# Gating of a mixture of experts in three operations instead of six, none of them on GpSimd

## The chip, the cores and the metric

The kernel runs on one core of a Trainium2 chip. The metric is the device time of one execution in microseconds (us). TensorE multiplies matrices, VectorE and ScalarE work on elements, GpSimd (Pool) does so too and issues the indirect transfers, SyncE issues most of the other transfers.

## What is computed

The reference runs two transformer-like blocks over 512 tokens of width 1024. The first block (two layers of convolution, a recurrent scan and a feed-forward) and the attention part of the second are not touched by the change. The part that matters here is the last stage, a mixture of 32 experts of which every token takes 4:

```python
u = (xb @ w1[e] + b1[e]).astype(jnp.float32)
glu = jnp.minimum(u[:, 0::2], SWIGLU_LIMIT)               # 7.0
lin = jnp.clip(u[:, 1::2], -SWIGLU_LIMIT, SWIGLU_LIMIT)
act = glu * jax.nn.sigmoid(SWIGLU_ALPHA * glu) * (lin + 1.0)   # alpha 1.702
y = act.astype(xb.dtype) @ w2[e] + b2[e]
return y.astype(jnp.float32) * g[:, None]
```

The even columns of `u` are the gate, the odd ones the linear part. The result is weighed by the token's gate, by a modulation row (`mod[:, 5]`, `M5` in the kernel) and added to the token.

## The kernel before

**One expert.** Experts are taken in a fixed order of rank by load. Each has a fixed number of rows (`CAPS`): rank 0 has 128, ranks 1 and 2 have 192 in two blocks, ranks 3 to 9 have 128, ranks 10 to 15 have 96, ranks 16 to 31 have 64. `ORDER` puts some 64-row experts first, then the two of 192, then those with 128, those with 96, and the other ten with 64. `up` (L1886) multiplies the gathered rows by the first matrix, 8 steps of 128 rows of weights (`kt`) into four PSUM banks `pu` of 512 columns; `down` (L1919) multiplies the gated result by the second into two banks `py`.

**Precision.** Each block of weights arrives by a transfer of 1 MB (`stage`, eight buffers in turn). `split_big` (L1782) makes of it a rounded copy `mh` on ScalarE (L1785) and the rest `ml` on VectorE (L1786); TensorE multiplies both parts (L1834). Up to 64 rows, a block is packed: the high and the low part of the rows lie side by side, and some steps (`PLAIN`) use the unsplit weights (L1829). The result of a packed block has two halves, which `whole` (L1840) joins with a copy on ScalarE and an addition on VectorE into SBUF; that of a wider block is read from PSUM as it is.

**Gating.** `gated` (L1874) works on one bank, 256 gate and 256 linear columns. VectorE clips the gate columns into `glu` (L1879) and the linear ones into a spare tile (L1880), ScalarE takes the Sigmoid (L1881), and Pool multiplies (L1882), adds 1 (L1883) and multiplies again (L1884). There are 34 blocks of rows and so 136 such units; in the second half of the last expert, two units, VectorE does Pool's part. Then `Rows(g, "a")` transposes `glu` on TensorE, eight transposes a block of rows (L1817), and copies them into two parts (L1819, L1821, L1822) for `down`.

**Order.** In the program text, the transposes of an expert's `glu` stand in the next expert's `up`, at `kt == 3`, and `down` after that; the rows of the next expert but one are gathered meanwhile (L1868, an indirect transfer that Pool issues), and results are added to the output by another (L1916). The text is not the final order. Before the run, the framework lays out the queue of each engine from its own estimates of durations, moving an instruction ahead of others where its inputs are expected; in the trace most transposes of `glu` stand earlier than `kt == 3`. At run time each engine takes its queue in order.

**Ahead of the experts.** L1772 to L1780 load the row `M5` and the biases of all experts and split the biases into a rounded part and a rest, `BB`, which is added by a matmul (L1838).

Of the kernel before, what the change touches and what calls it, by code (L numbers as in the profile page):

```python
# [16 lines left out]
AF = mybir.ActivationFunctionType  # L17
OP = mybir.AluOpType
# [10 lines left out]
CH = 64  # L29
STG = 8  # L30
ATC = 2
MB, LB = 3, 2

PLAIN = ((1, 4), (1, 2))
# [92 lines left out]
def tile_two_blocks(ctx: ExitStack, tc: tile.TileContext, I: dict, out: bass.AP, dump=None, stop=None):  # L127
    nc = tc.nc
# [16 lines left out]
    def bank(kind, shape, name):  # L145

        ring = dict(mm="AAAC", sq="BBDD", iv="A", pg="A", pp="B", py="C", sm="D", yy="B", tr="D", ad="A", s="EEE", w="F", o="G", t="HH", pv="I",
                    pre="EEEHH")[kind]
        turn[kind] = turn.get(kind, -1) + 1
        t = ring[turn[kind] % len(ring)]  # L150
        return ps.tile(shape or [128, 512], F32, name=name, tag="bank" + t, bufs=banks[t])

    def mmps(shape=None, name="mm"):
        return bank("mm", shape, name)
# [4 lines left out]
    def f32(ap):  # L159
        return ap.bitcast(F32)  # L160
# [541 lines left out]
    def scan(l, S):  # L702
# [66 lines left out]
        def conv_out(m):  # L769

            if m % 2 == 0 or not wcs:
                wcs[m // 2] = load_w(I["w_out"][l], 0, 4, (m // 2) * 256, 256)
            o = XT[:, m]
            if m < AHEAD_M:
                o = wk.tile([128, TT], F32, name="xm", tag="acc", bufs=1)
                nc.sync.dma_start(o[:, 0:w], xd[:, m * TT:m * TT + w])
            for i, (a, n) in enumerate(SEG[:1] if l == 1 else SEG):
                p = bank("pg", None, "pco")
                for kt in range(4):
                    nc.tensor.matmul(p[:, 0:n], lhsT=wcs[m // 2][:, kt, m % 2 * 128:m % 2 * 128 + 128], rhs=S["CV"][kt][:, a:a + n], start=kt == 0, stop=kt == 3)  # L780
                yield
                gated(o[:, a:a + n], p[:, 0:n], S["MOD"][:, i, 16 + m:17 + m], l == 1 and a < TX)
            if m < AHEAD_M:
                nc.sync.dma_start(xd[:, m * TT:m * TT + w], o[:, 0:w])
            yield
# [306 lines left out]
    def gated(o, src, gate, perm):  # L1092

        if perm:
            src = src.rearrange("p (c r) -> p r c", r=8)
            o = o.rearrange("p (r c) -> p r c", r=8)
        nc.vector.scalar_tensor_tensor(o, src, gate, o, op0=OP.mult, op1=OP.add)

    def proj_add(wsrc, nk, h, gates, both, perm, r0=0, after=None, parts=None):

        def add(m, p, a, n, gate):
            gated(XT[:, m, a:a + n], p[:, 0:n], gate[:, m:m + 1], perm and a < TX)

        for m2 in range(0, KT, 2):
            t = load_w(wsrc, r0, nk, m2 * 128, 256)
            if parts and m2 == KT - 2:
                ws = [split_w(t, i * 128, 128) for i in range(2)]
                ps_ = [[mmps(name="pp") for _ in parts] for i in range(2)]
                for j, (a, n) in enumerate(parts):
                    for i in range(2):  # L1110
                        mm3(ws[i], h, nk, [(ps_[i][j], a, n)], 128)
                        add(m2 + i, ps_[i][j], a, n, gates[a >= TX])
                continue
            for i in range(2):
                m = m2 + i
                sg = segs(both)
                mm3(split_w(t, i * 128, 128), h, nk, sg, 128)
                for s, (p, a, n) in enumerate(sg):
                    add(m, p, a, n, gates[s])
                if after:  # L1120
                    after(m)
# [128 lines left out]
    def win2(c0, n):  # L1250
        t = load_w(win, 0, KT, c0, n)
        return lambda i, m=128: split_w(t, i * 128, m)

    first = []
    with tc.high_priority():
        f = win2(256, 160)
# [24 lines left out]
    f = win2(0, 256)  # L1281
    for i in range(2):
        p_tile(f, i, 128, False, P1[:, i])
    f = win2(672, 256)
    for i in range(2):
        p_tile(f, i, 128, True, P1[:, 3 + i], 64 ** -0.5)
    f = win2(416, 256)
    for i in range(2):
        p_tile(f, i, 128, False, P1[:, 5 + i])
    for j in range(0, 4, 2):  # L1290
        f = win2(928 + j * 128, 256)
        for i in range(2):
            p_tile(f, i, 128, True, P2[:, j + i])
    for j in range(0, 4, 2):
        f = win2(1440 + j * 128, 256)
# [25 lines left out]
    for t in range(6):  # L1321
        p = bank("pre", None, "rvt")
# [63 lines left out]
    for t in range(4):  # L1386
        for a, n in SEG:
            p = bank("pre", None, "pq")
# [8 lines left out]
    p = bank("w", None, "ppe")  # L1397
# [9 lines left out]
    for t in range(6):  # L1407
        r = LAT[:, 4 + t:5 + t]
        for i in range(2):
            p = bank("pre", None, "pkv")  # L1410
# [14 lines left out]
    for t in range(4):  # L1425
        q = QT[:, t].rearrange("p (h c) -> p h c", h=8)[:, :, 64:96]
        o = wk.tile([128, 8, 32], F32, name="qpe", tag="qpe", bufs=1)
        turned(o, q, tables[0], t, 8)
        nc.scalar.activation(q, o, AF.Copy)
    for t in range(6):  # L1430
        rk = SS[:, 4 + t]
        k, kp = KTL[t], KP[:, t:t + 1]
        if t < 4:
            o = wk.tile([128, 1, 32], F32, name="kpe", tag="kpe", bufs=1)
            turned(o, kp, tables[1], t, 1)
        else:
            o = kp
# [137 lines left out]
    for h in range(4):  # L1575
        o = MO[:, 4 + h]
# [47 lines left out]
    def row_of(n, dst):  # L1624

        nc.scalar.dma_start(dst, bass.AP(tensor=CD.tensor, offset=CD.offset + n * D, ap=[[0, 128], [1, D]]))
# [12 lines left out]
    def stage(src, parts=1, eng=nc.sync):  # L1639
        t = stages[stages_used[0] % STG]  # L1640
        stages_used[0] += 1
        if parts > 1:
            t = t.rearrange("p (a b) -> p a b", a=parts)
        eng.dma_start(t, src)
        return t
# [28 lines left out]
    for t in range(4):  # L1674
        xr = XR[t // 2][:, t % 2]
        for c in range(2):
            p = mmps(name="prow")
# [84 lines left out]
    M5 = wk.tile([128, D], F32, name="M5")  # L1762
    XF = XT.rearrange("p k t -> p (k t)")
    spare = [XF[:, D * i:D * i + D] for i in range(6)]
    turn = dict(xg=0, y=0)

    def ring(kind):

        turn[kind] += 1
        return spare[2 * (kind == "y") + turn[kind] % 2]  # L1770

    row_of(2, M5)  # L1772

    BB = wk.tile([64, 3072], F32R, name="BB")
    bt = XF[0:32, 2 * D:5 * D]
    stages.extend(wk.tile([128, 2048], F32, name=f"st{i}") for i in range(6, STG))
    for src, c0, n in ((I["b_mlp1_2"][0], 0, 2048), (I["b_mlp2_2"][0], 2048, 1024)):
        nc.gpsimd.dma_start(bt[:, c0:c0 + n], src)
        nc.scalar.activation(BB[0:32, c0:c0 + n], bt[:, c0:c0 + n], AF.Copy)
        nc.vector.tensor_tensor(BB[32:64, c0:c0 + n], bt[:, c0:c0 + n], f32(BB[0:32, c0:c0 + n]), op=OP.subtract)  # L1780

    def split_big(t):  # L1782
        wh = wk.tile([128, 2048], F32R, name="mh", tag="mh", bufs=MB)
        wl = wk.tile([128, 2048], F32R, name="ml", tag="ml", bufs=LB)
        nc.scalar.activation(wh, t, AF.Copy)  # L1785
        nc.vector.tensor_tensor(wl, t, f32(wh), op=OP.subtract)  # L1786
        return wh, wl
# [83 lines left out]
    def glus(xs):  # L1871
        return [wk.tile([128, D], F32, name="glu", tag="glu", bufs=2)[0:x.m] for x in xs]

    def gated(x, p, i, glu, c, f, eng=nc.gpsimd):  # L1874

        u = x.whole(p, i).rearrange("p (f two) -> p two f", two=2)
        o = glu[:, c:c + 256]
        lin, sg = (spare[i][0:x.m, f:f + 256] for i in (4, 5))
        nc.vector.tensor_scalar(o, u[:, 0], 7.0, None, op0=OP.min)  # L1879
        nc.vector.tensor_scalar(lin, u[:, 1], 7.0, -7.0, op0=OP.min, op1=OP.max)  # L1880
        nc.scalar.activation(sg, o, AF.Sigmoid, scale=1.702)  # L1881
        eng.tensor_tensor(sg, o, sg, op=OP.mult)  # L1882
        eng.tensor_scalar(lin, lin, 1.0, None, op0=OP.add)  # L1883
        eng.tensor_tensor(o, lin, sg, op=OP.mult)  # L1884

    def up(w1, x, lb, out, at=(lambda kt: None)):  # L1886

        pu = [mmps(name=f"pu{n}") for n in range(4)]
        cols = [n * 512 for n in range(4)]
        for kt in range(KT):  # L1890
            if first:
                w = first.pop(0)
            else:
                t = early.pop(0) if early else stage(w1(kt))
                w = (t,) if x.packed and kt in PLAIN[0] else split_big(t)
            x.into(pu, w, kt, cols, [(lb, c) for c in cols], kt == KT - 1)
            at(kt)
        return [lambda n=n: gated(x, pu[n], n, out, n * 256, n * 256) for n in range(4)]

    def up_half(w1, xs, lb, h, out, at=(lambda kt: None)):  # L1900

        pu = [mmps(name=f"pu{n}") for n in range(2 * len(xs))]
        for j in range(KT // 2):
            w = split_big(stage(w1(j, h), 2).rearrange("p a b -> p (a b)"))
            for i in range(2):
                for b, x in enumerate(xs):
                    x.into(pu[2 * b:2 * b + 2], w, 2 * j + i, [i * 1024, i * 1024 + 512], [(lb, h * 1024), (lb, h * 1024 + 512)], j == 3 and i == 1)
                at(2 * j + i)
        return [lambda n=n: gated(xs[n // 2], pu[n], n, out[n // 2], h * 512 + n % 2 * 256, n * 256, nc.vector if len(xs) == 1 and h else nc.gpsimd) for n in range(2 * len(xs))]

    def weighed(y, x, p, n, c, tok, end):

# [168 lines left out]
    xs = [Rows(b[2], "x") for b in got[0][0]]  # L2081
    got[1] = place(ORDER[1])
    before, acts = None, []
    for i in range(33):
        steps = [None]
        if i < 32:
# [5 lines left out]
            out = glus(xs)  # L2092
# [15 lines left out]
        for step in steps:  # L2108
# [5 lines left out]
            for k in range(nparts):  # L2114
# [4 lines left out]
                if k < 2 and (i != 31 or not end):  # L2119
                    for _ in range((len(acts) + 1 - k) // (2 - k)):  # L2120
                        acts.pop(0)()
                if end and k == (ATC if nparts == 4 else 1) and i < 31:
                    xs = [Rows(b[2], "x") for b in got[i + 1][0]]
# [8 lines left out]
    with tc.For_i(0, nov, 1) as v:  # L2132
# [5 lines left out]
        x = Rows(xg, "x")  # L2138
        glu = glus([x])
# [36 lines left out]
```

## Time and profile before

| | |
|---|---|
| time, median of 3 runs | 4156.53 us (4144.9, 4156.53, 4166.9) |
| the profiled execution | 4152.49 us |
| its span, first to last instruction | 4150.5 us |
| mean granted clock of TensorE | 0.952 |
| busy: TensorE, VectorE, ScalarE, Pool | 92%, 68%, 41%, 21% of the span |
| the expert stage | from about 2740 us to the end |

Busy shares are means over very different stages. In the tables below, PE is TensorE, PEld its loading of weights, DVE VectorE, ACT ScalarE, POOL GpSimd, SP SyncE. Times are us from the start of the span, unless marked ns. PEclk is the clock that TensorE was granted, as a share of full speed. A row `out<-in` names the tiles that are written and read.

### The profile page before, as it was taken

Reading aid. Unit: us, or ns where it says so; the run is one execution under the profiler, and the core shown is the slowest. Engines: PE = TensorE matmul, PEld = TensorE weight load, DVE = VectorE, ACT = ScalarE, POOL = GpSimd, SP = SyncE. Lnnn points to the kernel's source line nnn. Section 1 sums busy time; section 2 is a strip of 40 time slices with the busy share of each in tenths; the row PEclk is TensorE's granted clock in tenths of the full one; section 3 lists DMA queues with packets and bytes.
Section 4 is the critical chain, followed back from the end, with each engine's and each line's share of the span. In section 5 each row is a group of like instructions: output and inputs, shape, how many; then the busy total and the mean of one; then the engine's idle time right before and its main releaser. Section 6 shows DMA issues by size and latency. Waiting matters only on the chain. (4 is left out here: it accounts for less than half of the span.)

```text
span 4150.5 us, 70327 instructions
## 1 busy us (share of the span) xinstructions
PE 3828.5 (92%) x27963; PEld 2860.0 (69%) x27963; DVE 2812.5 (68%) x5538; ACT 1710.6 (41%) x2552; POOL 873.9 (21%) x703
## 2 busy tenths in 40 slices
PE   7998999999999988999999989979999999888997
PEld 5777776888888777777878866754556776554343
DVE  4778875743434879867555545577687999677776
ACT  3233352321212334533222434445455766545554
POOL 0001110000000001110000000025566678545343
PEclk8999999999999999999999998989999999899899
DMA  5122423432322211125454310248697999778886
GB/s 200 53 70 65 133 54 104 133 119 85 122 81 92 73 48 33 41 60 164 156 160 129 77 51 1 107 176 309 242 339 277 365 360 348 270 274 311 300 334 219
DMA packets 353982, 677.90 MB, mean 163 GB/s; under 512 B 118759, under 2 KB 230194, under 8 KB 323538
## 3 DMA queue, kind: packets, MB, share of 16 engines
q1 hardware_dynamic: 343024, 636.89, 44.2%
q0 software_dynamic: 9376, 34.63, 3.4%
q8 instruction: 221, 3.62, 0.4%
q10 hardware_dynamic: 1250, 1.85, 0.1%
q14 instruction: 111, 0.91, 0.1%
HBM read 635.39 MB, written 37.90 MB: 162 GB/s over the span
## 5 line engine op out<-in xcount | busy, mean ns | idle before, releaser
L429 ACT ACTIVATE wh<-wst 128x1024 fp32r<-128x1024 f32 (+2 forms) x222 | 222.7, 1004 | 983.1 <-PE pc L439 524.3
L1786 DVE TENSOR_TENSOR ml<-E,mh 128x2048 fp32r<-128x2048 f32 x236 | 552.3, 2352 | 111.3 <-PE pu L1834 49.4
L1785 ACT ACTIVATE mh<-E 128x2048 fp32r<-128x2048 f32 x236 | 447.4, 1914 | 188.6 <-PE pu L1834 151.7
L439 PE MATMUL px<-Hh,wl 128*128 128x512 f32 (+2 forms) x1216 | 485.2, 399 | 13.9 <-DVE wl L430 13.7
L439 PE MATMUL px<-Hh,wh 128*128 128x512 f32 (+3 forms) x1216 | 484.5, 400 | 13.4 <-ACT wh L429 7.1
L439 PE MATMUL px<-Hl,wh 128*128 128x512 f32 (+3 forms) x1216 | 484.7, 399 | 1.0 <-DVE Hl L417 0.8
L430 DVE TENSOR_TENSOR wl<-wst,wh 128x1024 fp32r<-128x1024 f32 (+2 forms) x222 | 255.8, 1154 | 266.6 <-ACT wh L429 263.9
L1834 PE MATMUL pu<-ml,ch 128*64 128x512 f32 (+2 forms) x968 | 278.5, 406 | 20.5 <-DVE ml L1786 20.3
L1883 POOL TENSOR_SCALAR XT<-XT 64x256 f32<-64x256 f32 (+2 forms) x134 | 202.8, 1515 | 431.4 <-DVE XT L1880 414.5
L1834 PE MATMUL pu<-mh,ch 128*128 128x512 f32 (+1 forms) x968 | 282.5, 407 | 1.1 <-ACT ch L1819 1.0
L439 PEld LDWEIGHTS px<-Hh,wl 128*128 128x128 f32 (+1 forms) x1216 | 231.0, 190 | 72.6 <-DVE wl L430 18.9
L439 PEld LDWEIGHTS px<-Hh,wh 128*128 128x128 f32 (+1 forms) x1216 | 231.2, 191 | 72.0 <-ACT wh L429 9.4
L1006 POOL TENSOR_SCALAR XT<-XT,PC 128x64 f32<-128x64 f32 x160 | 85.3, 544 | 885.8 <-DVE XT L1009 370.7
L439 PEld LDWEIGHTS px<-Hl,wh 128*128 128x128 f32 (+1 forms) x1216 | 230.8, 190 | 56.8 <-DVE Hl L417 4.9
L531 DVE SCALAR_TENSOR_TENSOR acc<-ZC,VT,acc 128x272 f32<-128x272 f32 (+2 forms) x600 | 254.3, 485 | 2.6 <-ACT acc L526 2.5
L1786 DVE TENSOR_TENSOR ml<-st,mh 128x2048 fp32r<-128x2048 f32 x86 | 201.5, 2353 | 75.0 <-PE pu L1834 32.3
L1834 PEld LDWEIGHTS pu<-mh,ch 128*128 128x128 f32 (+1 forms) x968 | 174.4, 187 | 82.5 <-issue 31.7
L1834 PEld LDWEIGHTS pu<-ml,ch 128*64 128x64 f32 (+2 forms) x968 | 151.3, 161 | 91.3 <-DVE ml L1786 32.0
L1884 POOL TENSOR_TENSOR glu<-XT 64x256 f32<-64x256 f32 (+2 forms) x134 | 200.9, 1501 | 7.4
L439 PE MATMUL pc<-Hh,wh 128*128 128x256 f32 x672 | 193.3, 288 | 0.9 <-ACT Hh L416 0.9
L1882 POOL TENSOR_TENSOR XT<-glu,XT 64x256 f32<-64x256 f32 (+2 forms) x134 | 192.2, 1437 | 3.3 <-ACT XT L1881 3.2
L439 PE MATMUL pc<-Hl,wh 128*128 128x256 f32 x672 | 192.1, 286 | 0.5 <-DVE Hl L417 0.5
(599 smaller groups left out, 8487.2 us busy)
## 6 DMA issues: line engine op xcount, KB each, us to landing
E<-in_w_mlp_dram SPq DMA_DIRECT2D x288, 1024.0 KB
st<-in_w_mlp_dram SPq DMA_DIRECT2D x94, 1024.0 KB
wst<-in_w_in_dram SPq DMA_DIRECT2D x29, 1024.0 KB
adt<-in_ada_w_dram SPq DMA_DIRECT2D x96, 256.0 KB
adt<-in_w_ada_dram SPq DMA_DIRECT2D x96, 256.0 KB
wst<-in_ffn_wg_dram SPq DMA_DIRECT2D x22, 1024.0 KB
wst<-in_ffn_wu_dram SPq DMA_DIRECT2D x22, 1024.0 KB
adaw<-in_ada_w_dram SPq DMA_DIRECT2D x16, 1024.0 KB
```

Source lines behind the costliest of these rows:

```text
L429: nc.scalar.activation(wh, t[:, :, c0:c0 + n], AF.Copy)
L430: nc.vector.tensor_tensor(wl, t[:, :, c0:c0 + n], f32(wh), op=OP.subtract)
L439: nc.tensor.matmul(p[0:m, 0:n], lhsT=wa[:, k, 0:m], rhs=ha[:, k, a:a + n], start=k == 0 and first, stop=k == nk - 1 and last)
L531: nc.vector.scalar_tensor_tensor(o, z[:, j + a:j + a + n], cw(j), o, op0=OP.mult, op1=OP.add)
L1006: nc.gpsimd.tensor_scalar(M[:, 1], M[:, 0], PC[:, c:c + 1], None, op0=OP.mult)
L1785: nc.scalar.activation(wh, t, AF.Copy)
L1786: nc.vector.tensor_tensor(wl, t, f32(wh), op=OP.subtract)
L1834: nc.tensor.matmul(p[0:xa.shape[2]], lhsT=xa[:, kt], rhs=w[part][:, c:c + 512], start=kt == 0 and j == 0, stop=last and j == len(parts) - 1)
L1882: eng.tensor_tensor(sg, o, sg, op=OP.mult)
L1883: eng.tensor_scalar(lin, lin, 1.0, None, op0=OP.add)
L1884: eng.tensor_tensor(o, lin, sg, op=OP.mult)
```

## The change

`gated` takes Silu of 1.702 times the gate column on ScalarE straight from `u`, which is 1.702 times the gate times its sigmoid; VectorE clips the linear column to -6 and 8, and one scalar_tensor_tensor on VectorE limits the Silu to its value at 7 (`SILU7`) and multiplies by the linear part. For this the 1 of `lin + 1` goes into the bias of the odd columns, and the factor 1.702 is taken out again by dividing `M5` by it and multiplying the second bias by it. Each unit thus has one operation on ScalarE and two on VectorE, and none on Pool.

```diff
--- before.py
+++ after.py
@@ -29,6 +29,8 @@
 CH = 64
 STG = 8
 ATC = 2
+ALPHA = 1.702
+SILU7 = 7 * ALPHA / (1 + math.exp(-7 * ALPHA))
 MB, LB = 3, 2
 
 PLAIN = ((1, 4), (1, 2))
@@ -1769,13 +1771,20 @@
         turn[kind] += 1
         return spare[2 * (kind == "y") + turn[kind] % 2]
 
+
     row_of(2, M5)
+    nc.vector.tensor_scalar(M5, M5, 1.0 / ALPHA, None, op0=OP.mult)
 
     BB = wk.tile([64, 3072], F32R, name="BB")
     bt = XF[0:32, 2 * D:5 * D]
     stages.extend(wk.tile([128, 2048], F32, name=f"st{i}") for i in range(6, STG))
     for src, c0, n in ((I["b_mlp1_2"][0], 0, 2048), (I["b_mlp2_2"][0], 2048, 1024)):
         nc.gpsimd.dma_start(bt[:, c0:c0 + n], src)
+        odd = bt[:, 1:2048:2]
+        if c0:
+            nc.vector.tensor_scalar(bt[:, c0:c0 + n], bt[:, c0:c0 + n], ALPHA, None, op0=OP.mult)
+        else:
+            nc.vector.tensor_scalar(odd, odd, 1.0, None, op0=OP.add)
         nc.scalar.activation(BB[0:32, c0:c0 + n], bt[:, c0:c0 + n], AF.Copy)
         nc.vector.tensor_tensor(BB[32:64, c0:c0 + n], bt[:, c0:c0 + n], f32(BB[0:32, c0:c0 + n]), op=OP.subtract)
 
@@ -1871,17 +1880,14 @@
     def glus(xs):
         return [wk.tile([128, D], F32, name="glu", tag="glu", bufs=2)[0:x.m] for x in xs]
 
-    def gated(x, p, i, glu, c, f, eng=nc.gpsimd):
+    def gated(x, p, i, glu, c, f):
+
 
         u = x.whole(p, i).rearrange("p (f two) -> p two f", two=2)
-        o = glu[:, c:c + 256]
-        lin, sg = (spare[i][0:x.m, f:f + 256] for i in (4, 5))
-        nc.vector.tensor_scalar(o, u[:, 0], 7.0, None, op0=OP.min)
-        nc.vector.tensor_scalar(lin, u[:, 1], 7.0, -7.0, op0=OP.min, op1=OP.max)
-        nc.scalar.activation(sg, o, AF.Sigmoid, scale=1.702)
-        eng.tensor_tensor(sg, o, sg, op=OP.mult)
-        eng.tensor_scalar(lin, lin, 1.0, None, op0=OP.add)
-        eng.tensor_tensor(o, lin, sg, op=OP.mult)
+        o, lin = glu[:, c:c + 256], spare[4][0:x.m, f:f + 256]
+        nc.scalar.activation(o, u[:, 0], AF.Silu, scale=ALPHA)
+        nc.vector.tensor_scalar(lin, u[:, 1], 8.0, -6.0, op0=OP.min, op1=OP.max)
+        nc.vector.scalar_tensor_tensor(o, o, SILU7, lin, op0=OP.min, op1=OP.mult)
 
     def up(w1, x, lb, out, at=(lambda kt: None)):
 
@@ -1906,7 +1912,7 @@
                 for b, x in enumerate(xs):
                     x.into(pu[2 * b:2 * b + 2], w, 2 * j + i, [i * 1024, i * 1024 + 512], [(lb, h * 1024), (lb, h * 1024 + 512)], j == 3 and i == 1)
                 at(2 * j + i)
-        return [lambda n=n: gated(xs[n // 2], pu[n], n, out[n // 2], h * 512 + n % 2 * 256, n * 256, nc.vector if len(xs) == 1 and h else nc.gpsimd) for n in range(2 * len(xs))]
+        return [lambda n=n: gated(xs[n // 2], pu[n], n, out[n // 2], h * 512 + n % 2 * 256, n * 256) for n in range(2 * len(xs))]
 
     def weighed(y, x, p, n, c, tok, end):
```

## Rows read from the trace of the kernel before

**Rows 1.** List of waits, 2750 to 4151 us: us in total, times, longest.
```profile
PE pcol L1817 <- POOL glu L1884: 79.9, 39, 5.6
...
ACT XT L1881 <- DVE glu L1879: 73.2, 71, 2.6
```

**Rows 2.** List of waits, 2750 to 2950, 3474 to 3716, 3716 to 4088.
```profile
PE pcol L1817 <- POOL glu L1884: 19.3, 6, 5.6
...
PE pcol L1817 <- POOL glu L1884: 34.9, 13, 4.6
...
PE py L1834 <- DVE ml L1786: 4.3, 4, 1.2
...
PE pcol L1817 <- POOL glu L1884: 25.6, 19, 3.7
```

**Rows 3.** Table by stretch: us; busy us (x instructions); PEclk, DMA share, GB/s.
```profile
2740.00:2774.00 34.00, 10.28 (x43) 7.68 (x43) 31.60 (x86) 13.74 (x14) 16.47 (x13) 0.60 0.66 237
...
3214.00:3437.00 223.00, 223.00 (x1024) 176.46 (x1023) 216.52 (x214) 157.98 (x122) 158.85 (x82) 1.00 0.97 363
...
3763.00:4088.00 325.00, 295.67 (x966) 132.81 (x964) 237.81 (x271) 170.04 (x176) 140.80 (x112) 0.92 0.86 322
```

**Rows 4.** Timeline, a 96-row and a 64-row expert: start, us, instruction, [idle before <-releaser].
```profile
3547.82 0.41 DVE L1879 TENSOR_SCALAR glu<-pu 96x256 f32<-96x256 f32 x1
...
3556.38 0.39 PE L1817 MATMUL pcol<-CF,glu 96*128 96x96 f32 x2 [4.47 <-POOL glu L1884]
...
3965.70 0.34 PE L1817 MATMUL pcol<-CF,glu 64*128 64x64 f32 x2 [1.89 <-POOL glu L1884]
```

**Rows 5.** Table by stretches of 2 us behind that last wait.
```profile
3966.00:3968.00 2.00, 2.00 (x13) 1.03 (x11) 0.89 (x2) 1.92 (x5) 1.50 (x1) 0.68 0.97 387
3968.00:3970.00 2.00, 2.00 (x5) 0.73 (x4) 0.73 (x2) 2.00 (x3) 0.00 (x0) 0.50 1.06 291
3970.00:3972.00 2.00, 2.00 (x4) 0.67 (x4) 2.00 (x1) 2.00 (x2) 0.00 (x0) 0.50 0.37 92
3972.00:3974.00 2.00, 2.00 (x5) 0.47 (x4) 0.26 (x1) 1.53 (x1) 0.00 (x0) 0.62 0.04 8
```

**Rows 6.** Timeline of TensorE: the bias matmul near each expert's start.
```profile
3436.71 1.17 PE L1838 MATMUL pu<-BB,lb 64*96 64x512 f32 x4
...
3473.97 1.17 PE L1838 MATMUL pu<-BB,lb 64*96 64x512 f32 x4
...
3715.96 1.13 PE L1838 MATMUL pu<-BB,lb 64*64 64x512 f32 x4
...
4087.99 0.67 PE L1838 MATMUL pu<-BB,lb 64*64 64x512 f32 x2
```

**Rows 7.** Single lines of the kernel: duration ns min/median/max, first and last start, forms.
```profile
L1167 ACT ACTIVATE ft<-pc x22: 367/376/378, 785.0 to 1280.0; 128x256 f32<-128x256 f32 x22
L1167 ACT ACT_TABLE_LOAD  x3: 1283/1283/1283, 776.8 to 2223.4; - x3
...
L1786 DVE TENSOR_TENSOR ml<-E,mh x236: 2272/2289/2827, 2764.9 to 4120.5; 128x2048 fp32r<-128x2048 f32 x118
...
L1879 DVE TENSOR_SCALAR glu<-cl x72: 272/281/816, 2827.1 to 4124.4; 64x256 f32<-64x256 f32 x72
...
L1880 DVE TENSOR_SCALAR XT<-pu x64: 408/416/422, 2794.6 to 3695.5; 128x256 f32<-128x256 f32 x40, 96x256 f32<-96x256 f32 x24
...
L1882 DVE TENSOR_TENSOR XT<-glu,XT x2: 410/413/416, 4124.8 to 4125.7; 64x256 f32<-64x256 f32 x2
...
L1914 DVE SCALAR_TENSOR_TENSOR XT<-cl,ix,M x36: 733/738/1222, 2887.8 to 4138.0; 64x512 f32<-64x512 f32 x36
```

**Rows 8.** Timeline of ScalarE in a 128-row expert.
```profile
3310.32 1.90 ACT L1785 ACTIVATE mh<-st 128x2048 fp32r<-128x2048 f32 x1
3312.12 0.40 ACT L1881 ACTIVATE XT<-glu 128x256 f32<-128x256 f32 x1
```

**Rows 9.** The page, transfers: issues, KB each (the stage's other 96 are alike).
```profile
E<-in_w_mlp_dram SPq DMA_DIRECT2D x288, 1024.0 KB
```

## The prediction

> **What bounds the kernel now.** The kernel has many stages, so I read the waits before any share of busy time. In the expert stage (about 2740 us to the end) the list of waits [rows 1] shows which gaps of TensorE are named after the edited code: the transposes of `glu` at L1817 stood still 39 times, 79.9 us in all, for the last Pool operation of the gating, L1884. The reader is also to see the row below it: ScalarE waits 73.2 us for VectorE's first clip, L1879. ScalarE is not the bound, so that one is no price.
>
> Next, where these waits are. The same list cut into stretches [rows 2] gives 19.3 us in the first experts, 34.9 in the experts with 96 rows and 25.6 in the late ones with 64 rows: all of it. The table by stretch [rows 3] shows what limits where the waits are absent: from 3214 to 3437 us (128 rows) TensorE is busy all 223 us at full clock, VectorE 216.5 of 223, and the transfers run at 363 GB/s. From 3763 to 4088 us (64 rows) the clock is 0.92, VectorE is busy 73% and the transfers run at 322 GB/s: nothing there is full.
>
> Then one expert in order of time [rows 4]. In the 96-row expert VectorE begins the first clip at 3547.82, but the transposes of that block, for which TensorE had stood 4.47 us, start only at 3556.38: 8.5 us later, with the block's three Pool operations in between. In the 64-row experts the last block costs 1.89 us, and right behind it the granted clock falls [rows 5]: 0.68, 0.50, 0.50, 0.62 over four slices of 2 us. The lost clock is 2 x (0.32 + 0.50 + 0.50 + 0.38) = 3.4 us. A wait thus costs more than its length.
>
> **The change, part by part.** *Pool's three operations go.* There are 136 blocks of gating (72 packed with 64 rows, 64 wider), and 134 of them used Pool. What comes back is the wait plus the clock behind it, stretch by stretch.
>
> 96 rows: the starts of the experts [rows 6] give an undisturbed period, 3473.97 - 3436.71 = 37.3 us. The next five take 3715.96 - 3473.97 = 242.0 us, 55.7 us more than 5 x 37.3. Of this 4.3 us are waits for `ml` [rows 2], which stay. That leaves 51 us: the 34.9 of waits and half as much again for the clock. I take 46, leaving 1 us an expert for a shorter wait in the same place.
>
> 64 rows: nine experts from 3715.96 to 4087.99 take 41.3 us each [rows 6]. Waits 25.6 [rows 2], and nine falls of the clock at 3.4 [rows 5], 31, make 57 us, or 35.0 us an expert. (A clock of 0.92 over 325 us [rows 3] is 26 us in eight experts, the same size.) Each expert fetches 12 blocks of 1024 KB [rows 9], 12.6 MB; at 35.0 us that is 360 GB/s, as much as the best long stretch [rows 3]. I take three quarters, 43 us (36.6 us an expert, 344 GB/s), because the transfers would otherwise have to sit at that level throughout.
>
> First experts: 19.3 us of waits [rows 2]; the clock behind them is not counted; I take 15, since VectorE is also full of one-time work there. The gains add up to 46 + 43 + 15 = 104 us; everything at its full price would be 51 + 57 + 29 (19.3 with half again for the clock, as in the 96 rows) = 137. Nothing is taken for the 128-row experts, where TensorE has no gap to give back.
>
> *VectorE: one clip goes, one scalar_tensor_tensor comes.* The clip from SBUF takes 0.281, the one from PSUM 0.416 [rows 7]. The new operation has two SBUF inputs of 256 columns. The nearest rows are the product of L1882 on VectorE, 64 x 256, 0.413, below, and a scalar_tensor_tensor of 512 columns, 0.738, above [rows 7]. I take 0.47, close to the lower one, as the columns are the same. So 72 x 0.19 + 64 x 0.05 = 17 us more on VectorE; at the lower end 72 x 0.13 = 10, at the upper 72 x 0.46 + 64 x 0.32 = 54. The late experts leave VectorE a quarter of the time free [rows 3], and that is the cover; without it all 17 would show. I put a quarter, 4 us, on the path. Less Pool traffic should also speed VectorE: clips of median 0.281 reach 0.816 [rows 7]. I take nothing for it and keep it as the low end.
>
> The row says that the operation with two tensors is the dearer one, 0.413 against 0.281 at the same 64 x 256. The Trainium skill (VectorE: DVE Perf Modes, the perf-mode tier table) has the rule behind it, and it speaks against this change: an fp32 operation with one SBUF source can move two elements a cycle, one with two tensors cannot. By that page's formula for fp32 tensor_tensor the estimate is (256 + 151)/0.96 = 424 ns, and the sum would lie 1 us lower than with my 0.47.
>
> *ScalarE: Silu for Sigmoid.* The same count. A Silu from PSUM of 128 x 256 took 0.376 (22 of them), the Sigmoid 0.40 [rows 7, 8]; no cost. It no longer waits for VectorE's clip, as it reads PSUM (or the joined copy) itself. The clip and Silu can run side by side; the product on VectorE waits for both. Behind it in VectorE's queue stand the subtractions for `ml` (L1786), and TensorE waits for those. Cover is a Silu that is already done when the product comes up.
>
> *One-time work.* Three more operations on VectorE: the odd columns of the bias plus 1, the second bias times 1.702, M5 divided by it. From 0.3 us (a clip of 256 columns, 0.281) to 1.6 us (four times 0.413 for 1024 columns) [rows 7] each, so 1 to 5 us. VectorE is busy 31.6 of the 34 us there [rows 3], so little cover: I take 2 us, nearer the low end, as these have one tensor input. No transfer is added; the ones that exist keep their queues. Pool's gathers and scatters no longer stand behind gating; I take nothing for it.
>
> **The sum.** The profiled execution took 4152.5 us, 4 us below the median of the runs shown, 4156.5. 4152.5 - 104 + 4 + 2 = 4054.5, and 4 more for the median: **4058 us**.
>
> **Rivals.** *A, only part comes back (15 in 100).* The waits vanish but the clock still falls, because in the 64-row experts TensorE is choppy before the wait too, or the new waits on VectorE eat the difference. Then direct waits alone count: 4156.5 - 80 + 6 = 4083; with a third of the 39 waits left on VectorE, 4110.
>
> *B, the wait changes its name (7 in 100).* The queues are laid out before the run from estimates. If cheaper gating makes the planner put the transposes as much earlier as the result comes earlier, TensorE waits at L1817 for VectorE. A product that stands behind one `ml` subtraction is late by its 2.29 us [rows 7]; the mean wait now is 79.9/39 = 2.05 us. Time: about 4156. For it: the transposes already stand early. Against it: the result comes up to 8.5 us sooner [rows 4].
>
> *C, slower: VectorE held by Silu in the 128-row experts (7 in 100).* In that stretch VectorE has 6.5 us free for 24 blocks [rows 3], 0.27 us a block. ScalarE there runs a split of 1.90 us between two sigmoids [rows 8]. If the product comes up while Silu is behind a split, VectorE stands up to 1.9 us; 1.6 beyond its slack, 24 x 1.6 = 39 us, so 4058 + 39 = 4097. That alone is still faster. But if each such stop opens a gap of TensorE and the clock falls behind it as in [rows 5], it is 24 x (1.6 + 3.4) = 120 us, and the time is 4178. It decides at about 4.1 us a block (98/24), so only with the clock falling at nearly every block. Against it: the product can stand after the next subtraction, and Silu starts earlier than Sigmoid did.
>
> *D, tables (1 in 100).* If Silu and Copy did not live together on ScalarE, each of the 68 pairs of activations would want two loads of 1.283 us, 174 us on ScalarE, and with it on VectorE in part: some 4200. The 66 Silu of L1167, among copies, needed three loads [rows 7]. The Trainium skill (ScalarE: Activation LUTs, Table sets: the hidden batching unit) says that cheap functions such as copy are in every set; by that rule, too, there is one load, and the trace agrees.
>
> **How the numbers follow.** The likeliest case, waits and most of the clock come back, has 70 in 100: 4010 (all at full price, and some of VectorE's relief) to 4090. A spreads 4083 to 4130, B 4136 to 4170, C and D above. 0.5%, 21 us, is about what a measurement of this kernel can tell from no change; below 4136 lie the likeliest case and nearly all of A. Faster 0.84, same 0.08 (B and the upper edge of A), slower 0.08. A range from 4005 to 4115 leaves out B, C, D and a part of A, some 2 in 10.
>
> **What would show it.** Right: the row of waits of L1817 for `glu` gone or below 15 us under any name; periods of 37 to 39 us for all 96-row experts and 35 to 38.5 for the last 64-row ones; clock above 0.96 from 3500 us on; transfers near 345 GB/s there. Product 0.42 to 0.50. Wrong: a new row in which L1817 waits for VectorE's product with tens of us (B); VectorE's product waiting for Silu by more than 0.5 us a block, and a clock under 1.00 in the 128-row stretch (C); more than one table load in the stage (D); or the clock still falling in the late experts with no wait ahead of it (A). If transfers cannot hold 345 GB/s, SyncE's queue shows later landings and `mh` waits for a transfer.

## The result, and the profile after

| | before | after |
|---|---|---|
| median | 4157.97 us (4144.9 to 4166.9, 4 runs) | 4033.49 us (4022.44 to 4035.13, 4 runs) |
| span of the profiled execution | 4150.5 us | 4033.3 us |
| mean granted clock of TensorE | 0.952 | 0.961 |

The ratio of the times is 0.9697 (95% interval 0.9666 to 0.9729): 3.0% faster. The forecast of 4058 us was 24.5 us too high, inside its range. In the code of after, lines in and behind the gating stand 6 to 9 further down: Silu is L1888, the clip L1889, the product L1890, the split L1794 and L1795, the transposes L1826, the bias matmul L1847, the gather L1877.

The list of waits of after, 2740 to 4034 us (us in total, times, longest), has no row in which the transposes wait for `glu`, where [rows 1] had 79.9 us. The largest wait of TensorE in the stage is now one for `ml`:

```profile
PE pu L1843 <- DVE ml L1795: 20.9, 22, 1.7
...
PE pcol L1826 <- DMA XT<-HD,idx: 7.9, 2, 5.1
```

One expert of 96 rows shows why (timeline of after, columns as in [rows 4]). ScalarE takes the four Silu in a row, VectorE follows with clip and product, and the transposes come 4.1 us behind VectorE's first clip (6.9 behind the first Silu) with no wait in front of them; in [rows 4] it was 8.5 us from the first step of the gating, VectorE's clip, and a wait of 4.47.

```profile
3553.41 1.18 ACT L1888 ACTIVATE glu<-pu 96x256 f32<-96x256 f32 x4
3556.25 0.74 DVE L1889 TENSOR_SCALAR XT<-pu 96x256 f32<-96x256 f32 x2
...
3558.25 0.75 DVE L1890 SCALAR_TENSOR_TENSOR glu<-glu,XT 96x256 f32<-96x256 f32 x2
...
3560.30 0.53 PE L1826 MATMUL pcol<-CF,glu 96*128 96x96 f32 x4
```

The table by stretch of after (columns as in [rows 3]): the first experts (from 2774, which is 15.5 us ahead of their first bias matmul here), then those of 128, 96 and 64 rows.

```profile
2774.00:3197.00 423.00, 408.19 (x1625) 247.09 (x1624) 335.49 (x460) 245.88 (x242) 50.97 (x25) 0.96 0.84 314
...
3197.00:3419.00 222.00, 222.00 (x1022) 176.22 (x1020) 206.94 (x214) 156.88 (x122) 43.21 (x13) 1.00 0.96 366
...
3456.00:3645.00 189.00, 185.53 (x855) 126.27 (x854) 171.09 (x185) 125.28 (x102) 45.70 (x12) 1.00 0.95 353
...
3723.00:3969.00 246.00, 234.83 (x842) 109.00 (x841) 189.23 (x233) 150.50 (x154) 24.71 (x13) 1.00 0.99 369
```

Before, the same table for the 96-row experts and for the first ones:

```profile
3474.00:3716.00 242.00, 202.72 (x856) 135.16 (x855) 176.29 (x183) 128.04 (x102) 135.01 (x78) 0.90 0.77 278
2774.00:3214.00 440.00, 407.25 (x1598) 245.26 (x1598) 340.03 (x437) 238.52 (x235) 246.61 (x167) 0.95 0.80 294
```

In the 96-row experts the clock goes from 0.90 to 1.00 (the level of 2.4 GHz throughout) and the transfers from 278 to 353 GB/s; in the late 64-row ones from 0.92 [rows 3] to 1.00, and from 322 to 369. (The late stretch of [rows 3] holds eight periods and that of after seven; over the same eight, 3686.78 to 3968.87 us, after has a clock of 1.00 and 364 GB/s.) VectorE is busy for less time too, with as many instructions: 206.94 us in a 128-row stretch of 222, against 216.52 of 223. The late stretch now has the transfer share at 0.99: what limits there is the fetching of weights. No run took bytes away to show it, but pool_busy below puts almost five times the Pool work into that stretch without lengthening it.

The bias matmul near the starts of the experts, after:

```profile
2789.53 2.07 PE L1847 MATMUL pu<-BB,lb 64*128 64x512 f32 x4
...
3197.23 1.20 PE L1847 MATMUL pu<-BB,lb 64*128 64x512 f32 x4
...
3419.11 1.16 PE L1847 MATMUL pu<-BB,lb 64*96 64x512 f32 x4
...
3456.12 1.16 PE L1847 MATMUL pu<-BB,lb 64*96 64x512 f32 x4
...
3645.15 1.13 PE L1847 MATMUL pu<-BB,lb 64*64 64x512 f32 x4
...
3968.87 0.67 PE L1847 MATMUL pu<-BB,lb 64*64 64x512 f32 x2
```

and the two of before that [rows 6] lacks:

```profile
2774.17 1.20 PE L1838 MATMUL pu<-BB,lb 64*128 64x512 f32 x4
...
3214.45 1.20 PE L1838 MATMUL pu<-BB,lb 64*128 64x512 f32 x4
```

From these starts and [rows 6] the time can be split:

| stretch | before | after | gain | forecast |
|---|---|---|---|---|
| first bias to the 128-row experts | 440.3 | 407.7 | 32.6 | 15 |
| from there to the second 96-row expert | 259.5 | 258.9 | 0.6 | 0 |
| five 96-row periods | 242.0 | 189.0 | 53.0 | 46 |
| nine late 64-row periods | 372.0 | 323.7 | 48.3 | 43 |
| tail, to the end of the span | 62.5 | 64.4 | -1.9 | |
| start of the span to the first bias | 2774.2 | 2789.5 | -15.4 | -2 |

The last row is mostly not the change's: the last of it that no edit touches is already 12.6 us later in this execution (the first `pex` matmul of the routing, L1715 in after, starts at 2756.44 instead of 2743.79). The next run settles that.

### The profile page after: what moved, and what is told of

It is laid out like the page before. It is cut to its first block, busy times and chain, and to the rows that moved or that the text cites. A ratio compares the mean times of both kernels' runs of the same rounds, so it can differ in the third digit from the quotient of the medians.

```text
span 4033.3 us, 69782 instructions
## 1 busy us (share of the span) xinstructions
PE 3787.4 (94%) x27963; PEld 2847.6 (71%) x27963; DVE 2757.5 (68%) x5535; ACT 1707.5 (42%) x2552; POOL 330.9 (8%) x301
## 5 line engine op out<-in xcount | busy, mean ns | idle before, releaser
L1795 DVE TENSOR_TENSOR ml<-E,mh 128x2048 fp32r<-128x2048 f32 x236 | 536.1, 2286 | 92.0 <-PE pu L1843 44.3
L1794 ACT ACTIVATE mh<-E 128x2048 fp32r<-128x2048 f32 x236 | 447.7, 1916 | 187.6 <-PE pu L1843 147.5
L441 PE MATMUL px<-Hh,wl 128*128 128x512 f32 (+2 forms) x1216 | 485.9, 400 | 15.6 <-DVE wl L432 15.5
L1843 PE MATMUL pu<-ml,ch 128*64 128x512 f32 (+2 forms) x968 | 273.0, 399 | 21.1 <-DVE ml L1795 20.9
L441 PEld LDWEIGHTS px<-Hh,wl 128*128 128x128 f32 (+1 forms) x1216 | 231.0, 190 | 74.7 <-DVE wl L432 20.9
L1795 DVE TENSOR_TENSOR ml<-st,mh 128x2048 fp32r<-128x2048 f32 x86 | 196.0, 2286 | 42.8 <-PE pu L1843 24.5
L1843 PEld LDWEIGHTS pu<-ml,ch 128*64 128x64 f32 (+2 forms) x968 | 149.8, 159 | 90.7 <-DVE ml L1795 32.3
L441 PE MATMUL pc<-Hh,wl 128*128 128x256 f32 (+1 forms) x672 | 190.4, 284 | 0.1
L1794 ACT ACTIVATE mh<-st 128x2048 fp32r<-128x2048 f32 x86 | 163.2, 1917 | 55.4 <-PE pu L1843 31.7
L315 DVE SCALAR_TENSOR_TENSOR as<-adt,CS,as 128x512 f32<-128x512 f32 x224 | 161.3, 747 | 33.8 <-DMA adt<-in_w_ada_dram 19.4
L1099 DVE SCALAR_TENSOR_TENSOR XT<-px,MOD,XT 128x512 f32<-128x512 f32 x66 | 49.5, 750 | 188.9 <-PE px L441 188.6
```

The source lines that it names most:

```text
L315: nc.vector.scalar_tensor_tensor(acc[s], t, c, acc[s], op0=OP.mult, op1=OP.add)
L441: nc.tensor.matmul(p[0:m, 0:n], lhsT=wa[:, k, 0:m], rhs=ha[:, k, a:a + n], start=k == 0 and first, stop=k == nk - 1 and last)
L1843: nc.tensor.matmul(p[0:xa.shape[2]], lhsT=xa[:, kt], rhs=w[part][:, c:c + 512], start=kt == 0 and j == 0, stop=last and j == len(parts) - 1)
```

## The experiments

**again.** The changed kernel unaltered, beside the kernel before and the next three.

> The changed kernel once more, unaltered, as the measure for the others. If the later start of the expert stage in its first profile (12.6 us ahead of the first changed instruction) is chance, that offset changes here by several us while the stage itself, from its first transposes to the end, keeps its 1254 us within 6 us. If the change caused it, the stage starts late by 12 to 13 us again.

Measured: 4019.59 us against 4149.4, 0.9676 (0.9651 to 0.9701). The first bias starts at 2772.12 (timeline of TensorE), where it was 2789.53 in the first profile, and from there to the end it takes 1245.1 us (first profile 1243.8, before 1376.4).

```profile
2772.12 2.07 PE L1847 MATMUL pu<-BB,lb 64*128 64x512 f32 x4
```

So most of the late start was chance, and the expert stage gives back 131 to 133 us in both profiles. This run is the base for the runs below.

**six_on_vector.** The kernel before with its six operations, the three of Pool on VectorE instead: Pool is taken out of the chain, and nothing else is made cheaper.

```diff
-    def gated(x, p, i, glu, c, f, eng=nc.gpsimd):
+    def gated(x, p, i, glu, c, f, eng=nc.vector):
...
-        return [lambda n=n: gated(..., nc.vector if len(xs) == 1 and h else nc.gpsimd) ...]
+        return [lambda n=n: gated(...) ...]
```

> The old gating of six operations, with Pool's three always on VectorE. Theory W (TensorE stood for Pool's results and lost clock behind them; what counts is that Pool leaves this path): nearly all comes back, less the price of about 1.1 us more of VectorE a unit. The 128-row experts have 0.63 us a unit free on VectorE in the changed kernel (206.9 of 222 us busy, 24 units), so 0.47 x 28 = 13 us are lost there and 10 to 35 us in later waits for ml: 4055 to 4080. Rival N (the gain is the smaller number of operations, one fused product in place of four steps): 4130 or more, as VectorE now has all of them.

Measured: 4050.78 us, 0.9762 (0.9744 to 0.9781). No wait of TensorE for `glu` is left. So 99 of the 130 us come from taking the arithmetic off Pool, at the old count of operations. That takes it out of the chain, and also from beside VectorE and ahead of the gathers; the runs below tell these apart. The other 31 us is what VectorE's longer list costs: by [rows 7] it is 72 x 0.98 + 64 x 1.11 = 141 us more of VectorE's time than the changed kernel has (the gate's clip, two products and an addition, less the new product). In the table of busy time, where overlapping durations count once, it is 104 us more: 1120.9 from the first bias to the end, where again has 1016.7. So a quarter to a third of it shows. Of the loss, 13 us are in the 128-row experts, which take 39 us instead of 37.0, because VectorE is nearly full there (table by stretch, same columns):

```profile
3197.00:3393.00 196.00, 191.61 (x864) 148.66 (x863) 187.63 (x233) 132.19 (x102) 51.36 (x10) 1.00 0.92 344
```

More of it, 28 us, is in the first experts (435.0 us against 407.1), and the late 64-row ones are 10 us shorter than in again (315.4 against 325.5), nearly all of it in the first two, which take 37.1 and 33.4 us instead of 41.9 and 38.3. Why they are shorter stays open.

**two_on_pool.** The kernel before with the 1 in the bias and so without `lin + 1`: Pool keeps two operations a unit.

```diff
+        if not c0:
+            odd = bt[:, 1:2048:2]
+            nc.vector.tensor_scalar(odd, odd, 1.0, None, op0=OP.add)
...
-        nc.vector.tensor_scalar(lin, u[:, 1], 7.0, -7.0, op0=OP.min, op1=OP.max)
+        nc.vector.tensor_scalar(lin, u[:, 1], 8.0, -6.0, op0=OP.min, op1=OP.max)
...
-        eng.tensor_scalar(lin, lin, 1.0, None, op0=OP.add)
```

> The old kernel with one part of the change alone: the 1 goes into the bias and the clip becomes -6 to 8, so Pool has two operations a unit, and the third is left out. Theory W: each result is a third earlier, so the last waits of the 64-row experts (1.9 us behind a Pool chain of 10 us) vanish and the 96-row experts keep about 2 of 6 us: 4055 to 4105. If the gain goes with the time that Pool is busy (P), a third of it comes: about 4115.

Measured: 4070.15 us, 0.9812 (0.9791 to 0.9833). List of waits:

```profile
PE pcol L1820 <- POOL glu L1886: 36.0, 16, 4.3
```

One operation less on Pool takes away more than half of the 79.9 us. Of the 36.0, 10.3 are in the first experts, 18.9 in those of 96 rows and 6.9 in the first late expert of 64 rows, with three waits (the longest, from the timeline of TensorE):

```profile
3701.40 0.47 PE L1820 MATMUL pcol<-CF,glu 64*128 64x64 f32 x2 [3.67 <-POOL glu L1886]
```

That expert takes 46.8 us, hardly less than before (47.5). The eight behind it have no such wait, where before they had 17.2 us: there two operations are quick enough and three were not.

**last_on_pool.** The changed kernel with only the multiplication on Pool.

```diff
-        nc.vector.scalar_tensor_tensor(o, o, SILU7, lin, op0=OP.min, op1=OP.mult)
+        nc.vector.tensor_scalar(o, o, SILU7, None, op0=OP.min)
+        nc.gpsimd.tensor_tensor(o, o, lin, op=OP.mult)
```

> The changed kernel with only the last product on Pool: VectorE clips Silu at its limit (one tensor, 0.28 us) and Pool multiplies, one Pool operation a unit in the path instead of three. W: the four products of an expert end some 6 us after VectorE's clips instead of 10 to 14, which the margin of 5 to 8 us that the trace of before shows nearly covers: 4030 to 4060, waits for Pool below 20 us. If any Pool operation in the path cost as such, two thirds of the gain would be gone.

Measured: 4033.97 us, 0.9725 (0.9690 to 0.9760), an interval that overlaps those of the changed kernel. Its waits:

```profile
PE pcol L1826 <- POOL glu L1891: 7.9, 6, 3.2
```

With three, two, one and no operation of Pool in the chain the waits for `glu` are 79.9, 36.0, 7.9 and 0 us. The one operation is not free all the same: in its profile the stage takes 1259.1 us from the first bias to the end, 14 us more than again. The 128-row experts, which have no such wait, take 38.2 us instead of 37.0, and the last 96-row one 44.3 instead of 38.0.

**pool_in_path.** The changed kernel, and three operations of Pool between the product and the transposes, which together leave the value as it was.

```diff
+        sg = spare[5][0:x.m, f:f + 256]
+        nc.gpsimd.tensor_tensor(sg, o, o, op=OP.add)
+        nc.gpsimd.tensor_scalar(sg, sg, 0.25, None, op0=OP.mult)
+        nc.gpsimd.tensor_tensor(o, sg, sg, op=OP.add)
```

> The changed kernel with three Pool operations of the old kinds put between the product and the transposes (they give back the same values), so that TensorE must wait for them. Theory W (TensorE waited for Pool's results): the same Pool work that cost 66 us beside the path now costs most of the whole gain, 4110 to 4160, with 60 to 100 us of waits of the transposes of glu for Pool. Rival G (what Pool's work costs is the gathers queued behind it, not the results): as with that work beside the path, 4080 to 4095, and waits for gathers in place of waits for Pool's results.

Measured: 4153.64 us (10 runs), 1.0004 (0.9986 to 1.0021). The whole gain is gone, and both marks of the kernel before are back, the wait and the lost clock (list of waits; table by stretch of the late 64-row experts, to be laid beside [rows 3]):

```profile
PE pcol L1826 <- POOL glu L1894: 75.1, 29, 5.1
```

```profile
3765.00:4086.00 321.00, 287.49 (x960) 136.67 (x959) 228.42 (x266) 168.40 (x173) 136.18 (x111) 0.93 0.87 322
```

**pool_busy.** The changed kernel, and three operations of Pool behind the product whose result nobody reads: Pool is as busy as before, but not in the chain.

```diff
+        sg = spare[5][0:x.m, f:f + 256]
+        nc.gpsimd.tensor_tensor(sg, o, lin, op=OP.mult)
+        nc.gpsimd.tensor_scalar(sg, sg, 1.0, None, op0=OP.add)
+        nc.gpsimd.tensor_tensor(sg, lin, sg, op=OP.mult)
```

> The changed kernel, and Pool does three operations of the old shapes on each unit behind the product, whose result nobody reads. Theory W: Pool is as busy as before (some 800 us) and VectorE shares its ports with it again (subtractions at a mean near 2350 ns instead of 2286), but nobody waits for Pool: 4035 to 4055, waits of the transposes of glu below 5 us. Rival P (the gain is VectorE freed from Pool's traffic): back to 4120 to 4155.

Measured: 4085.74 us, 0.9852 (0.9829 to 0.9874): 66 us slower than again, and neither theory had that. There are no waits for `glu`, but another row has grown from 7.9 us:

```profile
PE pcol L1826 <- DMA XT<-HD,idx: 47.8, 7, 12.9
```

Pool's queue in a 96-row expert, and TensorE behind it (timelines):

```profile
3469.31 6.11 POOL L1893 TENSOR_SCALAR XT<-XT 96x256 f32<-96x256 f32 x2
3475.39 3.49 POOL L1894 TENSOR_TENSOR XT<-XT 96x256 f32<-96x256 f32 x2
3479.06 3.48 POOL L1926 DMA_INDIRECT out_dram<-XT,idx  x1 [0.17 <-issue]
3482.85 1.23 POOL L1877 DMA_INDIRECT XT<-HD,idx  x1 [0.30 <-issue]
```

```profile
3493.69 1.35 PE L1826 MATMUL pcol<-CF,XT 96*128 96x96 f32 x7 [12.85 <-DMA XT<-HD,idx]
```

The gather of the next rows is issued only when Pool is through with the dead arithmetic, and the transposes of those rows stop for 12.85 us. In the five 96-row periods such waits sum to 35.0 us, and the periods take 231.1 us instead of 189.0, so that a wait cost 1.2 times its length here. VectorE is as busy as in the kernel before (1076.2 us from the first bias to the end, before 1075.0, again 1016.7), and yet half of the gain is there. The late 64-row experts, on the other hand, keep their pace (245 us for the last seven periods, which again does in 245 too) with Pool busy 119.98 us in place of 24.70:

```profile
3772.00:4017.00 245.00, 233.85 (x838) 108.64 (x836) 200.67 (x231) 149.59 (x152) 119.98 (x95) 1.00 0.99 369
```

**pool_busy_not96.** The same without the dead work in the 96-row experts.

```diff
+        if x.m == 96:
+            return
         sg = spare[5][0:x.m, f:f + 256]
```

> The changed kernel with the three dead Pool operations per unit of pool_busy, but none in the experts of 96 rows. G (what cost pool_busy its 66 us was the gathers of the 96-row experts standing behind Pool's extra work, and the granted clock behind those waits): 4030 to 4045 us, the experts of 96 rows back to 37 to 38.5 us each, and waits of the transposes for gathers under 15 us. P (the price goes with the number of Pool operations beside VectorE): 112 of 136 units keep them, so 112/136 of 66 us, some 54, and about 4075 us. In both this kernel computes the same output as the changed one.

Measured: 4044.87 us, 0.9751 (0.9734 to 0.9767). Of the 66 us, 41 are gone with 24 of the 136 units, so it is the gathers that cost them and not the amount of Pool's work. The five 96-row periods are back at 3652.76 - 3463.75 = 189.0 us, as in after:

```profile
3463.75 1.16 PE L1847 MATMUL pu<-BB,lb 64*96 64x512 f32 x4
...
3652.76 1.13 PE L1847 MATMUL pu<-BB,lb 64*64 64x512 f32 x4
```

The remaining 25 us lie mostly in the first experts (2772.4 to 3201.84, 429.4 us against 407.7, and 407.1 in again), where the list of waits has 12.4 us for two gathers (after: 5.1 for one).

**pool_after_gather.** The changed kernel with twelve dead operations of Pool behind each gather, so that no gather stands behind them: a search for a price of Pool's work that is neither the chain nor the gather.

```diff
+        for f in range(0, D, 256):
+            d, s = spare[5][0:m, f:f + 256], M5[0:m, f:f + 256]
+            nc.gpsimd.tensor_scalar(d, s, ix[:, 7:8], None, op0=OP.mult)
+            nc.gpsimd.tensor_tensor(d, d, s, op=OP.mult)
+            nc.gpsimd.tensor_tensor(d, s, d, op=OP.mult)
```

> The changed kernel, and Pool does 12 operations of the old kinds after each gather that it issues, tied to that gather's index, on values nobody reads: as busy as before and on the shared ports, but neither in the path of glu nor ahead of the gather that TensorE needs next. W and G: 4020 to 4040, waits of the transposes for gathers below 12 us. P (VectorE's ports shared with Pool): 4080 or more, as when Pool was busy ahead of the gathers.

Measured: 4093.21 us, 0.9863 (0.9831 to 0.9896). My theory missed here. The gathers are in time (1.4 us of waits), but VectorE is slower. Its groups in the 128-row experts (busy us, mean ns of one), where after has 2288, 2287 and 415 ns:

```profile
L1795 DVE TENSOR_TENSOR ml<-E,mh 128x2048 fp32r<-128x2048 f32 x54 | 132.9, 2482 | 6.0 <-PE pu L1843 4.5 <-PE py L1843 1.1
L1795 DVE TENSOR_TENSOR ml<-st,mh 128x2048 fp32r<-128x2048 f32 x18 | 47.2, 2644 | 2.4 <-PE pu L1843 1.8 <-issue 0.4
L1895 DVE SCALAR_TENSOR_TENSOR glu<-glu,XT 128x256 f32<-128x256 f32 x24 | 16.2, 714 | 0.0
```

VectorE was nearly full there, and the period rises from 37.0 to 40.0 us. TensorE's waits for `ml` in the stage go from 20.9 to 46.5 us (row of `pu`) and from 5.1 to 24.8 (row of `py`). A part of the 74 us is of the experiment's own making, since VectorE's index and routing steps share a tile with the dead work: TensorE stands 14.27 us for `ml` behind such a step, and once, ahead of the first bias, 17.67 us for `SELP`. The rest shows a second price of Pool's work: VectorE's own operations last longer beside it. It is 3 us an expert with 128 rows and with 96 (40.6 for 37.8), and less than 1 us in the late ones (36.8 for 36.2). Why twelve operations in a row cost the 128-row experts more than the same number spread out in pool_busy (37.4 to 37.5 us) stays open.

**onetime_on_pool.** The three one-time operations on Pool (two runs).

```diff
-    nc.vector.tensor_scalar(M5, M5, 1.0 / ALPHA, None, op0=OP.mult)
+    nc.gpsimd.tensor_scalar(M5, M5, 1.0 / ALPHA, None, op0=OP.mult)
```

and the same for the other two.

> The changed kernel with its three one-time operations on Pool instead of VectorE. They took 0.67 us each on VectorE. If they cost the 3 us by which the first bias now comes later behind the first transposes (9.9 us instead of 6.8), this distance falls back to 7 or 8 us; the time as a whole moves less than a measurement can tell.

Measured: 4021.23 us, 0.9683 (0.9647 to 0.9720), not to be told from again. From the first transposes to the first bias it takes 7.2 us (2767.48 to 2774.68), where again has 9.99 and before 6.81. But two of the three (2747.88 to 2753.96) now stand in Pool's queue ahead of operations whose result the first gather reads, and TensorE's wait for that gather is 6.7 us instead of 5.0. No version of these runs beats the changed kernel.

## Why the prediction was right, step by step

**The waits of L1817 and the clock behind them: right, and mis-sized by a quarter.** The price of a wait was put at half as much again (96 rows) to 2.2 times (64 rows) its length. Measured, 34.9 us of waits were worth 53.0 (1.5 times), 25.6 worth 48.3 (1.9 times), and pool_in_path gave 134 us for 75.1 of waits (1.8 times). These are means over uneven experts: the first late one had 8.4 us of waits and gave back 5.9, the eight behind it 17.2 and 42.4. The terms that were mis-sized are 46, where 51 stood at full price and 53.0 came; 43, "three quarters" of 57, where 48.3 came, so that the full price was too high there; and 15 for the first experts, where 32.6 came. The reserve for the late experts, that the transfers would otherwise "have to sit at that level throughout", was not needed: 369 GB/s over 246 us.

**First experts: 32.6 instead of 15.** Part of the gap is a step that was costed at nothing: "Pool's gathers and scatters no longer stand behind gating; I take nothing for it". In the kernel before, the two gathers at 3075 us came right behind a row of gating operations (timeline of Pool):

```profile
3074.13 0.81 POOL L1884 TENSOR_TENSOR glu<-XT 64x256 f32<-64x256 f32 x1
3075.11 5.84 POOL L1868 DMA_INDIRECT XT<-HD,idx  x1 [0.17 <-issue]
3081.26 0.93 POOL L1868 DMA_INDIRECT XT<-HD,idx  x1 [0.30 <-issue]
```

and the transposes that they feed stood still (timeline of TensorE):

```profile
3090.58 0.69 PE L1817 MATMUL pcol<-CF,XT 128*128 128x128 f32 x2 [5.99 <-DMA XT<-HD,idx]
```

That expert took 42.2 us before (3067.46 to 3109.66) and takes 33.6 now: 8.6 us. pool_busy and pool_busy_not96 show the same mechanism with larger numbers. The other 24 us are not shown to be the 19.3 of waits with a quarter for the clock: 6.9 of these waits stood in the first expert, whose period hardly changed (32.6 us before, 32.5 after), and pool_busy_not96, which has no wait for `glu`, is 22 us slower there than again. How much of the 24 belongs to the waits, and how much to VectorE beside a quiet Pool, stays open.

**VectorE: 17 us more forecast, 58 us less measured.** The product was put at 0.47 us, and its lower bound, 0.413, was the true one (from the changed kernel, duration of one in ns, min/median/max):

```profile
L1890 DVE SCALAR_TENSOR_TENSOR glu<-glu,XT x136: 406/411/421, 2815.5 to 4007.2; 64x256 f32<-64x256 f32 x72, 128x256 f32<-128x256 f32 x40, 96x256 f32<-96x256 f32 x24
```

So by the medians the exchange costs 72 x 0.13 = 9 us of VectorE, not 17; by the sums of all durations it is 2 us (54.0 for the clips that went, 56.0 for the products). Against it stands the relief that I took nothing for: 236 subtractions for `ml` went from a mean of 2352 to 2286 ns, 15.6 us, and shorter operations gained as well. From the first bias to the end VectorE is busy 1016.7 us, where it was 1075.0. The 4 us on the path were thus a term with the wrong sign, and small. The assumption that a quarter of VectorE's extra work shows fits six_on_vector (31 of 141, or of 104 by busy time), where VectorE is fuller than here. The relief is not the main part of the gain: pool_busy takes it back and is 64 us faster than the kernel before, and pool_busy_not96 104 us.

**ScalarE and rivals C and D: refuted.** Silu takes 384 ns from PSUM and 434 from the joined copy, there is one table load, and VectorE's product waited for Silu four times, 3.8 us in all, its clip four times, 6.1 us (the same view, of L1888; the last two rows are who waited):

```profile
L1888 ACT ACTIVATE glu<-cl x72: 414/434/443, 2844.2 to 4006.5; 64x256 f32<-64x256 f32 x72
L1888 ACT ACTIVATE glu<-pu x64: 368/384/406, 2812.6 to 3631.5; 128x256 f32<-128x256 f32 x40, 96x256 f32<-96x256 f32 x24
...
L1888 ACT ACT_TABLE_LOAD  x1: 1283/1283/1283, 2811.2 to 2811.2; - x1
...
  DVE XT L1889: 6.1, 4
  DVE glu L1890: 3.8, 4
```

**Rivals A and B: refuted.** The clock is 1.00 in both stretches where it fell before, and 0.98 in the 78 us between them (the first two late experts), so little of it stayed away. The planner did not use the earlier results up: no row of waits for `glu` has come under another engine's name.

**One-time work: 3 us for 2.** The operations take 0.67 us each, 2.0 in all as forecast; the distance from the first transposes to the first bias went from 6.81 to 9.89, 3.1 us. The rest of the 15.4 us at that place was chance, as again showed: the first bias starts anywhere from 2762.9 to 2789.5 us in the eleven profiles.

**The balance in spans.** Forecast 4150.5 - 104 + 4 + 2 = 4052.5, measured 4033.3. The stretches behind the first bias gave 132.6 where 104 - 4 = 100 was forecast, 32.6 more; ahead of it 15.4 was lost where 2 was forecast, 13.4 more. The difference is 19.2. So luck made the number look better than the sum was: without the late start, as in again, the time is 4019.59 us, 38 below the forecast.

Of the signs named ahead, some were missed: the product was just below the 0.42 to 0.50, and of the nine late periods the first takes 41.6 us (41.9 in again), over the 38.5, and the last 32.3, under the 35; between them one takes 36.7 and six take 35.3 to 35.6. In the first, TensorE waits 2.5 us for `ml` and 2.78 for a gather; whether that is all of its length no run shows. The transfers ran at 369 GB/s, above the 345.

## What to carry to other kernels

A short wait of TensorE had no fixed price here: 1.5 times its length over the 96-row experts, 1.9 over the late ones (0.7 in the first of them, 2.5 in the rest), 1.2 for the gathers of pool_busy. Price it from undisturbed periods of the same work, as was done for the 96 rows (51 us at full price, 53.0 measured), rather than from the waits times a factor, and do not round that price down. When work leaves an engine that also issues indirect transfers, list the transfers that stood behind it in that engine's queue and ask which consumer was late for them. Taking the arithmetic off the slow engine gave three quarters of the gain with no operation saved; shortening the list for the other engine gave the rest, part of it where that engine was nearly full.

## What the runs showed of the hardware

Pool's and VectorE's operations stretch each other. A product on Pool over 256 columns had a median of 0.74 us before and a longest of 6.10; in pool_busy one operation lasts 5.77. In the other direction, in pool_after_gather, a product of VectorE of 0.415 us had a mean of 0.714, and single subtractions of 2.29 reached 5.35. The Trainium skill (SBUF — State Buffer, Terms) says that the two engines share a port pair which is held for a whole instruction, so that the loser blocks fully. The trace agrees for Pool: of its 402 gating operations before, 276 took under 1.25 us, 122 took 2 us or more, and 4 lay between. VectorE's subtractions before were not lengthened by multiples: 272 of 322 took under 2.4 us and the rest at most 2.83. Which instruction held the ports in each case the profile does not show.

Pool's work behind the product did no harm in the late 64-row experts (245 us with it and without it) and cost 41 us in the 96-row ones, where gathers stood behind it. Three operations ahead of the transposes cost 134 us over the stage. Most of the price of work on Pool came from what stood behind it and not from its length; the rest came through VectorE, as in pool_after_gather.
